# Longer read runs, a second queue at the start, and split first and last stores in a DMA-bound rotation kernel

## The chip, the core and the metric

The kernel runs on one core of a Trainium2 chip. The metric is device time in microseconds (us), the median of several runs. The profile comes from one further execution of each kernel; its span is about 1.8 us shorter than the time of that execution.

Engines in this text: DVE is the vector engine, which does the transposes. SP and ACT are the sync and scalar engines; here they only issue DMAs, each on a hardware queue of its own (q1 is SP's, q10 is ACT's in the profile). Sixteen DMA engines move the bytes of both queues.

## The reference

```python
def setup_inputs():
    batch, c, h, w = 32, 3, 256, 256
    return {"x": np.random.randn(batch, c, h, w).astype(np.float32)}

def reference(x):
    return np.rot90(x, k=1, axes=(-2, -1)).astype(np.float32)
```

96 images of 256 x 256 float32 are rotated: 25.17 MB are read and 25.17 MB are written. There is no arithmetic.

## The kernel before

Four images make a tile of 128 partitions x 2048 elements (8 KB of each partition, 1 MB in all). There are 24 tiles. Each is loaded with 8 KB runs, transposed on DVE with reversed access patterns, and stored with 8 KB runs.

```python
    in_pool = ctx.enter_context(tc.tile_pool(name="in_pool", bufs=12))
    out_pool = ctx.enter_context(tc.tile_pool(name="out_pool", bufs=12))

    for g in range(N // Q):                      # 24 tiles
        S = in_pool.tile([P, R * W], fp32, name="S")
        nc.sync.dma_start(out=S[:], in_=x_v[g])  # load, SP's queue
        U = out_pool.tile([P, R * W], fp32, name="U")
        # ... (the reversed views src of S and dst of U)
        nc.vector.transpose(dst, src)
        nc.scalar.dma_start(out=o_v[g], in_=U[:])  # store, ACT's queue
```

The scheduler gives the DMAs eight semaphores in turn, loads and stores together, in the order in which it schedules them. A DMA may be issued only when the DMA that held its semaphore before has landed. The compiled program shows it as waits. These are SP's loads in the kernel before (output of the build, semaphores numbered 0 to 7; the semaphores in the trace agree):

```
SP:  load 0 to load 4   no wait
     load 5             waits for semaphore 0   (load 0)
     load 6             waits for semaphore 2   (load 2)
     load 7             waits for semaphore 4   (load 3)
     load 8             waits for semaphore 6   (load 4)
     ...
```

In this program every load from load 5 on waits for an earlier load. The stores wait for earlier stores, except two (the fourth and the last but one), which take over the semaphore of a load that landed long before.

## Time and profile before

| | before |
|---|---|
| time, median of 3 runs | 124.34 us |
| profiled span | 122.7 us |
| DVE busy | 94.4 us (24 x 3.96 us) |
| bytes at the plateau of 427 GB/s | 117.9 us |

The page of the kernel before. In the slice rows each entry is one of 40 equal slices of the span; the first two rows are busy tenths.

```profile
span 122.7 us, 162 instructions
...
DVE  0199999999896696886976968879669688696600
...
DMA  3999999999999999999999999999999999999995
GB/s 88 419 427 411 312 430 433 422 433 427 427 427 427 427 427 427 427 427 427 427 427 427 427 427 427 427 427 430 427 427 427 427 427 427 427 427 427 427 427 211
...
DMA S<-in_x_dram 73%; DMA out_dram<-U 13%; DVE U L40 6%; SPq L35 1%; DVEq L40 0%
...
S<-in_x_dram SPq DMA_DIRECT2D x24, 1024.0 KB, 19.6
out_dram<-U ACTq DMA_DIRECT2D x24, 1024.0 KB, 16.5
```

The DMA engines are full from the second slice to the last but one: this kernel is bound by transfer. Only the first slice, the fifth (312 GB/s) and the last are low. The last two lines give the DMAs' median time from issue to landing.

### The profile page before, as it was taken

The page shows a single profiled execution, that of the slowest core. Times are in us where ns is not written, and L with a number is a line of the kernel's source. Part 1 is how long each engine was busy: PE and PEld are TensorE (multiplying, and loading weights), DVE is VectorE, ACT ScalarE, POOL GpSimd, SP SyncE. Part 2 cuts the span into 40 slices and gives each one's busy share as a digit, 9 for nine tenths or more (in the row PEclk, how much of TensorE's full clock was granted, in tenths as well). Part 3 has the DMA queues.
Part 4 walks back from the last instruction along what each step waited for, and adds up shares of the span by engine and source line. Part 5 has one row for each costly group of instructions (what it writes and reads, how often), then busy time and mean ns, then how long its engine had stood idle before and what let it go on. Part 6 is the DMA issues. An engine that isn't in the chain of part 4 may idle for free.

```text
span 122.7 us, 162 instructions
## 1 busy us (share of the span) xinstructions
DVE 94.4 (77%) x24; POOL 0.2 (0%) x4
## 2 busy tenths in 40 slices
DVE  0199999999896696886976968879669688696600
POOL 0000000000000000000000000000000000000000
DMA  3999999999999999999999999999999999999995
GB/s 88 419 427 411 312 430 433 422 433 427 427 427 427 427 427 427 427 427 427 427 427 427 427 427 427 427 427 430 427 427 427 427 427 427 427 427 427 427 427 211
DMA packets 6912, 50.33 MB, mean 410 GB/s; under 512 B 768, under 2 KB 768, under 8 KB 768
## 3 DMA queue, kind: packets, MB, share of 16 engines
q1 hardware_dynamic: 3456, 25.17, 49.6%
q10 hardware_dynamic: 3456, 25.17, 48.5%
HBM read 25.17 MB, written 25.17 MB: 410 GB/s over the span
## 4 chain that ended last, share of the span: by engine, by line
DMA 86%; DVE 6%; SPq 1%; issue 0%; DVEq 0%
DMA S<-in_x_dram 73%; DMA out_dram<-U 13%; DVE U L40 6%; SPq L35 1%; DVEq L40 0%
## 5 line engine op out<-in xcount | busy, mean ns | idle before, releaser
L40 DVE STREAM_TRANSPOSE U<-S 128x2048 f32<-128x2048 f32 x24 | 94.4, 3958 | 21.2 <-DMA S<-in_x_dram 20.2
L56 POOL MEMSET const-uint8-127<- 128x1 uint8 x1 | 0.1, 102 | 0.0
L56 POOL MEMSET const-bfloat16-1.0<- 128x1 bf16 x1 | 0.1, 101 | 0.0
L56 POOL MEMSET const-float32-0.0<- 128x1 f32 x1 | 0.1, 98 | 0.2 <-issue 0.2
L56 POOL MEMSET const-float32-1.0<- 128x1 f32 x1 | 0.1, 98 | 0.0
## 6 DMA issues: line engine op xcount, KB each, us to landing
S<-in_x_dram SPq DMA_DIRECT2D x24, 1024.0 KB, 19.6
out_dram<-U ACTq DMA_DIRECT2D x24, 1024.0 KB, 16.5
```

Of the source, the lines that this page charges most:

```text
L35: nc.sync.dma_start(out=S[:], in_=x_v[g])
L40: nc.vector.transpose(dst, src)
L56: nc = _bacc.Bacc("TRN2", target_bir_lowering=False, num_devices=1)
```

## The change

The intent: fewer, longer reads; a faster start through a second queue; finer first and last stores.

```diff
+    FOLD = 32
+    FIRST, LAST = 4, 2
+    xv = xf.rearrange("(n d f) -> n d f", n=G, d=FOLD)   # 32 runs of 32 KB
+    def load(dst, src):
+        nc.sync.add_instruction(mybir.InstDMACopy(
+            ins=[nc.sync.lower_ap(src, opt=False)],      # [32, 8192]
+            outs=[nc.sync.lower_ap(dst, opt=False)],     # [128, 2048]
+            queue="qSPDynamicHW", ... ))
...
-        nc.sync.dma_start(out=S[:], in_=x_v[g])
+        if n == 0:
+            nc.sync.dma_start(out=S, in_=xp[n])
+        elif n == 1:
+            nc.scalar.dma_start(out=S, in_=xp[n])
+        else:
+            load(S, xv[n])
...
-        nc.scalar.dma_start(out=o_v[g], in_=U[:])
+        pieces = FIRST if n == 0 else LAST if n == G - 1 else 1
+        f = F // pieces
+        for i in range(pieces):
+            nc.scalar.dma_start(
+                out=op[n, :, i * f : (i + 1) * f], in_=U[:, i * f : (i + 1) * f])
```

So tile 0 is stored by four DMAs of 256 KB in 2 KB runs, and tile 23 by two DMAs of 512 KB in 4 KB runs. The transpose walks the same elements in another order.

More of the change, by code (lines that the diff above doesn't have):

```diff
@@ L21 @@
     R = 8
-    K = H // R
-    Q = P // K
+    F = R * W
+    G = N // 4
+    FOLD = 32
+    FIRST, LAST = 4, 2
     fp32 = mybir.dt.float32
-    x_v = x.rearrange("b c (k r) w -> (b c k) (r w)", r=R).rearrange("(g p) f -> g p f", p=P)
-    o_v = out.rearrange("b c (k r) w -> (b c k) (r w)", r=R).rearrange("(g p) f -> g p f", p=P)
-    in_pool = ctx.enter_context(tc.tile_pool(name="in_pool", bufs=12))
-    out_pool = ctx.enter_context(tc.tile_pool(name="out_pool", bufs=12))
-    for g in range(N // Q):
-        S = in_pool.tile([P, R * W], fp32, name="S")
-        nc.sync.dma_start(out=S[:], in_=x_v[g])
-        U = out_pool.tile([P, R * W], fp32, name="U")
-        src = S.rearrange("p (r k q) -> p q r k", r=R, q=R)[:, ::-1, :, ::-1]
-        dst = U.rearrange("p (q k r) -> p q r k", q=R, r=R)
-        nc.vector.transpose(dst, src)
-        nc.scalar.dma_start(out=o_v[g], in_=U[:])
+    xf = x.rearrange("b c h w -> (b c h w)")
@@ new lines @@
+    of = out.rearrange("b c h w -> (b c h w)")
+    xp = xf.rearrange("(n p f) -> n p f", p=P, f=F)
+    op = of.rearrange("(n p f) -> n p f", p=P, f=F)
+    s_pool = ctx.enter_context(tc.tile_pool(name="S", bufs=12))
+    u_pool = ctx.enter_context(tc.tile_pool(name="U", bufs=12))
+    xv = xf.rearrange("(n d f) -> n d f", n=G, d=FOLD)
+    def load(dst, src):
+        nc.sync.add_instruction(
+            mybir.InstDMACopy(
+                name=nc.get_next_instruction_name(),
+                engine=mybir.EngineType.SP,
+                ins=[nc.sync.lower_ap(src, opt=False)],
+                outs=[nc.sync.lower_ap(dst, opt=False)],
+                queue="qSPDynamicHW",
+                mode="Copy",
+            )
+        )
@@ new lines @@
+    for n in range(G):
+        S = s_pool.tile([P, F], fp32, name="S")
+        U = u_pool.tile([P, F], fp32, name="U")
+        if n == 0:
[4 more added lines that the diff above has]
+            load(S, xv[n])
+        nc.vector.transpose(
+            U.rearrange("p (q k r) -> p r q k", q=R, r=R),
+            S.rearrange("p (r k q) -> p r q k", r=R, q=R)[:, :, ::-1, ::-1],
+        )
+        pieces = FIRST if n == 0 else LAST if n == G - 1 else 1
+        f = F // pieces
+        for i in range(pieces):
+            nc.scalar.dma_start(
+                out=op[n, :, i * f : (i + 1) * f], in_=U[:, i * f : (i + 1) * f]
+            )
```

## The prediction

> **What bounds it now.** The DMA engines. In the page's 40 slices the DMA row is 9 almost throughout, at 427 GB/s; 50.33 MB at 427 GB/s are 117.9 us of the 122.7 us span. DVE is busy 94.4 us (24 transposes of 3.96 us) and waits 20.2 us for loads: it follows. In the stretch table 14.5 to 110 us runs at 427 GB/s (loads and stores about 214 each, by the DMA records), and 110 to 121 us, stores alone, also at 427. So the tail is transfer too: the last store is issued at 115.6 us while earlier ones still run.
>
> The 4.8 us that are not full-rate transfer: (a) first issue at 0.73 us, first packet at 1.74, full rate from about 3.0; (b) 11.5 to 14.5 us runs at 314 instead of 427 GB/s, which loses 0.8 us. Load packets there take 400 to 700 ns instead of 309, and the first store, issued on ACT at 9.7 us, has its first packet at 13.9 us; no later store shows this. I take it for the cold start of the ACT queue. (c) 1.2 us after the last packet.
>
> **What the change does.**
> 1. Second load on ACT: ACT's queue starts cold at 0.7 us, beside SP's. If (b) is that cold start, it mostly overlaps (a). Worth at most 0.8 us; I take 0.6.
> 2. 22 loads read 32 KB runs: 2 read runs per engine for 8. An 8 KB packet starts every 306 ns; 256 beats of 32 B at 850 MHz are 301 ns. The Trainium skill, "DMA: Bandwidth & Descriptors", section "Why small descriptors are slow (HBM only)", gives about 3 cycles of overhead per packet, which agrees with the 5 ns here. Estimate: 22 x 6 x 5 ns = 0.65 us if packets count by reads; nothing if by the 8 KB writes. I take 0.4.
> 3. The same page ("Queues, rings and completion order") says that an engine switches queues at packet boundaries. With 32 KB load packets against 8 KB stores, loads may get far more than half: 214/214 would tilt towards 340/85, loads and DVE would end much earlier, and a long stretch of stores alone would follow. The bytes are the same and some queue always has work, so this moves time and saves none. Semaphores keep at most 4 loads and 4 stores in flight.
> 4. First store in four pieces of 2 KB runs, last in two of 4 KB: 24 + 8 more packets per engine, 5 ns each: costs 0.15 us; the extra issues on ACT (0.34 us each) are hidden.
> 5. The transpose's access order changes, same 2048 elements; DVE has slack, so even 10% would be hidden.
>
> Sum: -0.6 - 0.4 + 0.15, and some -0.3 for a faster start with two queues issuing: about -1.2 us, nearly all on the critical resource, since every byte waits for it.
>
> **Prediction.** 123.1 us, 80% range 122.0 to 124.3. Faster by over 2% (below 121.85): 0.10. Within 2%: 0.87. Slower by over 2%: 0.03.
>
> **What would show it.** Step 1: no slice of about 312 GB/s near 12 us. Step 2: fewer, 32 KB load packets, and a plateau of 430 to 433. Step 3: uneven shares, loads landed well before 110 us, DVE done earlier. Step 4: still about 1.2 us after the last packet. Step 5: transposes near 3.96 us.
>
> **What would make it wrong.** If 32 KB reads into 4 partitions lose the spread over the engines or stall writes, the plateau falls and it is slower. If the reads' overhead were larger than 5 ns, the plateau could reach 435 and the time fall to 121. If the dip belongs to the first writes to DRAM rather than to the queue, step 1 gains nothing.

The 5 ns per packet in this text are an assumption of the prediction. The traces give about 3.7 ns (see step 2 at the end).

## More of the kernel before

What SP's queue waits for, in the kernel before (total us, times, longest us):

```profile
SPq L35 <- DMA S<-in_x_dram: 81.8, 19, 4.6
SPq L67 <- DMA out_dram<-U: 29.5, 4, 22.3
```

The first line is the semaphore waits of the loads: each waits for a load, and loads land regularly. The second is the wait at the end of the program (line 67 is the launch, not a load).

## The result, and the profile after

| | before | after |
|---|---|---|
| time, median of 6 runs each | 124.35 us | 125.34 us (125.02 to 125.83) |
| ratio | | 1.0085, 95% interval 1.0062 to 1.0109 |
| profiled span | 122.7 us | 123.9 us |

A ratio is the mean time of one kernel's fast runs over that of the other's fast runs of the same rounds, so it is not quite the ratio of the medians. The change makes the kernel 0.85% slower: clear of the noise, but within 2%. The prediction was 123.1 us, with a range that ended at 124.3.

The same lines of the page, after:

```profile
span 123.9 us, 168 instructions
...
DVE  0039999999999999999999999918999993000000
...
DMA  3999979999999999999999999999999999999992
GB/s 87 423 505 413 434 244 412 378 436 442 436 439 436 428 410 399 450 407 442 439 423 452 439 423 439 386 391 428 428 428 426 434 423 426 426 428 431 423 414 118
...
DMA out_dram<-U 56%; DVE U L62 17%; DMA S<-in_x_dram 6%; DVEq L97 3%; DVEq L62 0%; ACTq L69 0%
...
S<-in_x_dram SPq DMA_DIRECT2D x23, 1024.0 KB, 13.1
out_dram<-U ACTq DMA_DIRECT2D x22, 1024.0 KB, 10.8
```

The low fifth slice is gone. In its place are low slices at the sixth (244) and the eighth (378). A packet counts where it starts, so slices with 32 KB packets scatter (505 is such an artefact). DVE ends much earlier, and the chain now runs through stores: the loads are done at 83 us, not 111.

To avoid that artefact I spread each DMA record evenly over its duration, and added up the time lost against 428 GB/s. Loss = length of the stretch x (1 - rate / 428). The last column is a run explained below.

| stretch, us | before | after | first store whole |
|---|---|---|---|
| 0 to 3.5 | 2.68 | 2.64 | 2.52 |
| 3.5 to 15 | 0.89 | 0.04 | 0.07 |
| 15 to 24 | 0.02 | **1.40** | 0.35 |
| 24 to 118 | 0.12 | 0.03 | 0.02 |
| 118 to the end | 1.41 | **2.21** | 1.44 |
| sum | 5.12 | 6.32 | 4.40 |

The start gains nothing. The dip before the first store moved from 11.5 to 15 us with the first store itself. Between 18 and 24 us there is a new loss, and the end is longer: the sixteen engines' last completion records lie 0.55 us apart before (121.01 to 121.56) and 1.28 us apart after (121.32 to 122.60). If each engine has a fixed share of the bytes, the one that lost most ends last. The kept records carry no engine number, so this was not checked.

What happens at 18 to 24 us is told by the waits of SP's queue and by its issues. First its waits, after:

```profile
SPq L97 <- DMA out_dram<-U: 51.8, 1, 51.8
SPq L40 <- DMA S<-in_x_dram: 47.4, 15, 7.6
SPq L40 <- DMA out_dram<-U: 10.8, 3, 8.5
```

The third line is new: loads (line 40) wait three times, up to 8.5 us, for a **store**. Then SP's issues between 5 and 19 us and between 19 and 21 us, after (start, length, what, count):

```profile
10.59 0.47 SPq L40 DMA_DIRECT2D S<-in_x_dram  x1
...
19.62 1.77 SPq L40 DMA_DIRECT2D S<-in_x_dram  x2
```

From 11.1 to 19.6 us SP issues nothing. The load at 10.59 is load 5; the one at 19.62 is load 6. The compiled program says why:

```
SP after:  load 0, 2, 3, 4   no wait          (load 1 is on ACT)
           load 5            semaphore 2  (load 2)
           load 6            semaphore 4  (piece 0 of the first store)
           load 7            semaphore 6  (piece 2 of the first store)
           load 8            semaphore 0  (piece 3 of the first store)
```

Piece 0 was issued at 12.14 us, and the last of its 16 completions came at 19.61 us. Load 6 followed at 19.62, and its first packet came at 23.0 us. But the load queue had emptied at 18.5 us: no load packet runs from 18.5 to 23.0 us. In the last part of this gap the store packets that ran alone became slow. The records of one DMA engine, joined by their times (start ns, length ns; the 2 KB packets of the pieces are left out):

```
13796  1251  load, 32 KB
15047  1236  load, 32 KB
16273  1696  load, 32 KB      slow: the first pieces begin
20475   309  store, 8 KB
20781   309  store, 8 KB
21087   309  store, 8 KB
21393   309  store, 8 KB
21699   309  store, 8 KB
22004   384  store, 8 KB      slow, although no other queue runs
22384   434  store, 8 KB
22815   381  store, 8 KB
23199  1572  load, 32 KB      load 6 begins
```

### The profile page after: what moved, and what is told of

The parts are those of the page before. It is cut to its first block, busy times and chain, and to the rows that moved or that the text cites. A ratio compares the mean times of both kernels' runs of the same rounds, so it can differ in the third digit from the quotient of the medians.

```text
span 123.9 us, 168 instructions
## 1 busy us (share of the span) xinstructions
DVE 92.3 (74%) x24; POOL 0.2 (0%) x4
## 4 chain that ended last, share of the span: by engine, by line
DMA 62%; DVE 17%; DVEq 3%; issue 0%; ACTq 0%
DMA out_dram<-U 56%; DVE U L62 17%; DMA S<-in_x_dram 6%; DVEq L97 3%; DVEq L62 0%; ACTq L69 0%
## 5 line engine op out<-in xcount | busy, mean ns | idle before, releaser
L62 DVE STREAM_TRANSPOSE U<-S 128x2048 f32<-128x2048 f32 x24 | 92.3, 3945 | 11.1 <-DMA S<-in_x_dram 8.1
## 6 DMA issues: line engine op xcount, KB each, us to landing
out_dram<-U ACTq DMA_DIRECT2D x22, 1024.0 KB, 10.8
```

Source lines behind the costliest of these rows:

```text
L62: nc.vector.transpose(U.rearrange("p (q k r) -> p r q k", q=R, r=R), S.rearrange("p (r k q) -> p r q k", r=R, q=R)[:, :, ::-1, ::-1],)
```

## The experiments

Sixteen kernels ran, all correct. "Gap" is the longest stretch of at least 1 us without a load packet before the last load ends, from the DMA records. Times are medians.

| run | time, us | ratio to before | gap in the loads, us |
|---|---|---|---|
| before | 124.35 | | none |
| after | 125.34 | 1.0085 | 18.5 to 23.0 |
| e1 first store whole | 123.78 | 0.9948 | none |
| e2 no 32 KB runs | 125.71 | 1.0101 | 18.7 to 22.7 |
| e3 load 1 on SP | 125.30 | 1.0069 | 16.4 to 21.1 |
| e4 last store whole | 125.34 | 1.0077 | 18.2 to 22.8 |
| e5 first store one DMA, 2 KB runs | 123.90 | 0.9955 | none |
| e6 first store four DMAs, 8 KB runs | 123.99 | 0.9968 | none |
| b2 before + four pieces | 125.70 | 1.0103 | 16.4 to 20.5 |
| b3 before + 32 KB loads | 123.96 | 0.9964 | none |
| e7 pieces, six loads ahead | 124.67 | 1.0021 | 23.5 to 28.2 |
| e9 pieces, eight loads ahead | 124.59 | 1.0018 | 31.2 to 36.8 |
| e8 no pieces, loads 5 and 6 late | 124.23 | 0.9987 | none |
| e11 no pieces, load 5 very late | 125.09 | 1.0053 | 15.4 to 17.8 |
| e10 whole, eight ahead | 123.81 | 0.9960 | none |
| b7 before, eight ahead | 124.36 | 1.0002 | none |
| b5 before, three input buffers | 126.38 | 1.0169 | none |
| b6 before, one queue | 125.14 | 1.0063 | none |

### First: which part of the change costs

Theory A: the four pieces of the first store. Theory B: the 32 KB packets. Each run undoes one part.

**e1**, first store whole.

```diff
-    FIRST, LAST = 4, 2
+    FIRST, LAST = 1, 2
```

> The changed kernel with its first store in one piece. Theory A (the four pieces of 2 KB runs crowd out the sixth load and bring on the second slow stretch at 21 to 24 us, which also leaves the 16 engines' ends 1.3 us apart): about 124.0 us, no second slow stretch, engines end within 0.7 us of each other. Theory B (the 32 KB load packets themselves slow the stretch and scatter the engines): unchanged, 125.3 us, engines still over 1.2 us apart.

Measured: 123.78 us (123.73 to 123.82), 0.5% faster than before. The engines end 0.52 us apart. Theory A holds: the pieces cost 1.6 us, and without them the change is a gain. Waits of SP's queue in this run:

```profile
SPq L97 <- DMA out_dram<-U: 55.7, 4, 48.4
SPq L40 <- DMA S<-in_x_dram: 52.5, 18, 5.6
SPq L40 <- DVE U L62: 0.9, 2, 0.4
```

No load waits for a store any more.

The table of stretches shows 14 to 24 us too (the stretch, its length, DVE busy, POOL busy, clock, DMA share, GB/s). The kernel before:

```profile
14.00:24.00 10.00, 10.00 (x3) 0.00 (x0) 1.00 1.01 423
```

The changed kernel:

```profile
14.00:24.00 10.00, 10.00 (x4) 0.00 (x0) 1.00 0.99 352
```

And e1:

```profile
14.00:24.00 10.00, 10.00 (x4) 0.00 (x0) 1.00 0.99 406
```

The DMA share hides the difference (0.99 in both of the last two), because a slow packet counts as busy. The rate shows it.

**e2**, all loads in 8 KB runs.

```diff
-            load(S, xv[n])
+            nc.sync.dma_start(out=S, in_=xp[n])
```

> The changed kernel with all loads in 8 KB runs. Theory A: still slow, 125.2 to 125.6 us (the 0.3 us of the longer packets is lost, the crowding stays). Theory B: 124.3 us or less, engines end within 0.6 us, no stretch under 400 GB/s after 19 us.

Measured: 125.71 us, and the gap is there. Theory B falls. The 32 KB runs are worth about 0.4 us (125.71 - 125.34) in this setting.

**e3**, the second load back on SP.

```diff
-            nc.scalar.dma_start(out=S, in_=xp[n])
+            nc.sync.dma_start(out=S, in_=xp[n])
```

> The changed kernel with the second load back on the sync queue. The prediction's step 1 (cold ACT queue) would have the dip before the first store larger by 0.6 us and the time at 125.9; if the dip belongs to the first store whatever the queue did before, the dip stays 0.7 to 0.8 us and the time within 0.2 us of 125.3.

Measured: 125.30 us. The loss from 11 to 15 us is 0.72 us there, against 0.71 us from 15 to 18.5 us in the changed kernel. So an ACT queue that has already carried a load does not spare the dip: it comes with the first store, and the second load's queue is worth nothing. That refutes step 1 of the prediction. It agrees with the Trainium skill, "DMA: Bandwidth & Descriptors", section "Issuing engines are not separate DMA queues", which says that DMAs of all issuing engines run on the same 16 DMA engines and that a second one saves only the time to issue. In the changed kernel the first landing is even later, because two loads share the engines: DVE begins at 8.12 us, against 5.57 in e3 and 5.72 before. The comparison of e3 with the changed kernel has the gap on both sides. Without a gap, e1 and b3 below differ by 0.18 us (123.78 against 123.96) in the second load's queue, the split last store and the order of the transpose together, so the second queue may be worth up to about that there.

**e4**, last store whole.

```diff
-    FIRST, LAST = 4, 2
+    FIRST, LAST = 4, 1
```

> The changed kernel with its last store in one piece of 8 KB runs. 8 more packets of 5 ns per engine are 0.04 us and one DMA fewer completes: 125.3 us, within 0.1. If the two last DMAs add to the tail, 124.9 or less.

Measured: 125.34 us (124.91 to 125.91). The two last pieces are worth nothing either way.

### Second: what in the four pieces costs

**e5**, one DMA that moves the same 2 KB runs.

```diff
+        if n == 0:     # one DMA on ACT
+            ins=[nc.scalar.lower_ap(U.rearrange("p (i f) -> p i f", f=f), opt=False)]
+            outs=[nc.scalar.lower_ap(op[n].rearrange("p (i f) -> p i f", f=f), opt=False)]
```

> The changed kernel with its first store as ONE DMA that still moves 2 KB runs (512 of them). It separates what the four pieces cost: if the 2 KB packets (their number) crowd the sixth load out, 125.0 to 125.4 us, as with four pieces, and the sixth load starts near 23 us; if the number of DMAs handed to the scalar queue does, about 123.9 us (0.12 us for the small packets above the whole store), and the sixth load starts directly after the fifth, near 18 us.

Measured: 123.90 us. Small packets alone do not cost it.

**e6**, four DMAs in 8 KB runs.

```diff
+        if n == 0:
+            for i in range(4):
+                nc.scalar.dma_start(out=op[n, i::4, :], in_=U[i::4, :])
```

> The changed kernel with its first store as FOUR DMAs of 256 KB in 8 KB runs (every fourth partition). The mirror of the run before: if the number of DMAs crowds the load out, about 125.2 us and the sixth load starts after 22 us; if the 2 KB packets do, 123.8 to 124.0 us and it starts near 18 us.

Measured: 123.99 us. Four DMAs alone do not cost it either. Both of my either-or readings had failed. In e1, e5 and e6 the loads up to load 5 are issued by 3 us and load 6 near 9.3 us. In the changed kernel load 5 goes at 10.6 and load 6 at 19.6. The scheduler had handed out the semaphores in another order. In e6 six loads took theirs in the first eight, in the changed kernel only five, and the next load inherited that of a piece.

**b2**, the kernel before with the four pieces only.

```diff
-        nc.scalar.dma_start(out=o_v[g], in_=U[:])
+        pieces = 4 if g == 0 else 1
+        f = R * W // pieces
+        for i in range(pieces):
+            nc.scalar.dma_start(out=o_v[g][:, i * f : (i + 1) * f], in_=U[:, i * f : (i + 1) * f])
```

> The kernel before with nothing but the four pieces of the first store. If the pieces alone make the loss, whatever the load's runs: 124.4 + 1.4 = about 125.7 us. If they hurt only together with the 32 KB loads or the second load on the scalar queue: 124.4 to 124.6 us.

Measured: 125.70 us, as theory A said: the pieces hurt by themselves, with 8 KB loads too. Again loads wait for the store (11.4 us in 3 waits), and the gap is there. But most of the 1.3 us is lost elsewhere. This is the row of rates of b2's page, to be compared with that of the kernel before:

```profile
GB/s 85 426 423 431 306 408 404 431 426 428 431 423 431 423 423 433 428 426 431 428 426 428 426 423 431 428 428 431 428 423 431 426 423 431 428 428 428 428 291 211
```

The last slice but one has 291 GB/s instead of 427. By the spread records, the stretch from 3.5 to 24 us loses 0.35 us more than before, and that from 118 to 121 us 0.98 us more. The late loads shift the rest of the program: the last load lands at 115.1 us instead of 111.5, the last store is issued at 119.2 instead of 115.6, and by then the stores before it are nearly done, so the engines run short of work. In the changed kernel the loads are done at 83 us and this does not happen; its loss at the end goes mostly with the uneven ends. So b2 confirms the delay of the loads, not the same sum of losses.

**b3**, the kernel before with the 32 KB loads only.

```diff
+        if g >= 2:     # the raw copy of the change, SP's queue
+            ins=[nc.sync.lower_ap(xv[g], opt=False)], outs=[nc.sync.lower_ap(S, opt=False)]
```

> The kernel before with nothing but the 32 KB loads (from the third on). From the packets' measured spacing (1217 ns for 32 KB, 1224 ns for four of 8 KB, 44 per engine) 0.3 us: 124.05 us; with the leave-one-out difference of the two runs above (125.34 - 125.71) 0.4 us. The prediction had 0.4. If longer packets unbalance the engines, 124.4 or more.

Measured: 123.96 us, ratio 0.9964 (0.9951 to 0.9977): about 0.45 us of gain, close to the predicted 0.4.

### Third: is it the load queue running dry

Theory C: the pieces harm only through their semaphores, which make a load late, so that the load queue runs dry. Theory D: four DMAs of 2 KB packets harm as such.

**e7**, all pieces kept, but six loads scheduled before them. The edit hoists the loads and adds an ordering for the scheduler, which is no wait in the program.

```diff
+    for n in range(AHEAD):          # AHEAD = 7
+        fetch(n)
...
+            tc.keep_in_program_order(s)
+            if n == 0:
+                tc.add_manual_dep(s.ins, loads[5].ins.name, <order only>, reason="order")
```

> The changed kernel with its four 2 KB pieces kept, but scheduled after load 5 (an order for the scheduler, no wait), so that six loads, not five, take their semaphores before the pieces do; load 5 is then issued near 3 us instead of 10.6, load 6 near 10.6 instead of 19.6. Theory C (the pieces harm only by taking the eight DMA semaphores, so that loads 5 to 8 are issued late and the sync queue runs dry from 18 to 23 us): 123.9 to 124.1 us, no stretch without load packets before 60 us. Theory D (four DMAs of 2 KB packets together harm by themselves): 125.2 us or more.

Measured: 124.67 us, between the two. The gap was not removed, it moved to 23.5 to 28.2 us: load 8 now held the semaphore of piece 0, which landed at 24.15 us; so load 8 was issued at 24.16 us, and its first packet came at 28.2 us. Waits of SP's queue in e7:

```profile
SPq L40 <- DMA S<-in_x_dram: 46.1, 14, 6.9
SPq L40 <- DMA out_dram<-U: 9.1, 2, 8.2
```

Piece 0 took 12.1 us to land here. Its 2 KB packets get one or two turns after each 32 KB load packet: 84 ns against 1,240 in the records (medians). The better the loads run, the later a small store piece lands, and the load behind it pays.

**e8**, no pieces, but loads 5 and 6 made late through their buffers.

```diff
-        S = s_pool.tile([P, F], fp32, name="S")
+        S = (t_pool if n in (0, 1, 5, 6) else s_pool).tile([P, F], fp32, name="S")
```

> The kernel with the first store whole (123.78 us), but loads 5 and 6 put into the buffers of tiles 0 and 1, so that they are issued late, near 11.7 and 15.5 us, as the pieces made them. Theory C: the sync queue runs dry near 18 us and the time rises by 0.5 us or more, to 124.3 to 125.3. Theory D: no piece is there, 123.8 us.

Measured: 124.23 us (124.05 to 124.31). That is 0.45 us slower than e1 without any piece, just short of the 0.5 that I had expected at least, and no full gap opened. It counts for theory C, weakly.

After these runs the theory was likely but not shown: every run with a gap had pieces.

**e9**, pieces kept, eight loads ahead of them.

```diff
-    AHEAD = 7
+    AHEAD = 8
-                    loads[5].ins.name,
+                    loads[7].ins.name,
```

> The changed kernel, all four 2 KB pieces and the two last ones kept, but scheduled so that eight loads take their semaphores before the first piece does. Theory C: no gap in the load packets before 60 us, 123.9 to 124.1 us. Theory D: 125 us or more though the loads never run dry. If a gap only moves once more, 124.6.

Measured: 124.59 us, the third of the three outcomes. The gap moved once more, to 31.2 to 36.8 us: load 11 was issued at 32.78 us, when the third piece had landed at 32.77 us.

Waits of SP's queue in e9:

```profile
SPq L40 <- DMA S<-in_x_dram: 42.5, 11, 10.9
SPq L40 <- DMA out_dram<-U: 10.7, 2, 8.3
```

So I found no schedule of the four pieces without a gap, and theory C was not confirmed from this side. What e9 adds is that the loss travels with the gap: from 3.5 to 30 us it loses 0.15 us in all, although the pieces are issued from 12.3 us on and the last lands at 33.7 us; from 30 to 40 us it loses 0.68 us. How long the gap is does not set the loss: 4.6 us of gap stand beside 1.6 us lost in the changed kernel, 5.6 us beside 0.8 in e9 (both against e1).

**e11**, no pieces, and load 5 alone forced to be very late.

```diff
-        S = s_pool.tile([P, F], fp32, name="S")
+        S = (t_pool if n in (1, 5) else s_pool).tile([P, F], fp32, name="S")   # t_pool: 1 buffer
```

> The kernel with the first store whole (123.78 us), no pieces, but load 5 put into the buffer of tile 1, so that it is issued near 15.5 us, when the fifth load is nearly done. Theory C: the load packets have a gap of 3 to 5 us near 18 us, and the time is 124.5 to 125.3. Theory D: 123.8 us.

Measured: 125.09 us (124.15 to 125.73), 1.3 us above e1. The one thing that differs is a load that waits for DVE (and the loads that queue behind it on SP), as the waits of SP's queue in e11 show:

```profile
SPq L41 <- DMA S<-in_x_dram: 49.1, 16, 6.4
SPq L41 <- DVE U L63: 7.0, 3, 6.3
```

The profiled execution is the fastest of the six (124.15 us); its gap, 15.4 to 17.8 us, is shorter than I had expected. The scatter is wide. In this execution the stretch of the gap shows no extra loss (0.31 us from 15 to 24 us, against 0.35 in e1); it is 0.37 us slower than e1 in all. No slow execution was profiled. So it is shown that a late load costs time without any piece, in all six runs; that the dry queue makes the whole 1.3 us of the median is argued, not seen. Theory D had 123.8 us here and falls as the whole explanation; e9's loss before 30 us leaves little for the pieces by themselves.

### Fourth: the dip before the first store, and a better version

**b5**, the kernel before with three input buffers.

```diff
-    in_pool = ctx.enter_context(tc.tile_pool(name="in_pool", bufs=12))
+    in_pool = ctx.enter_context(tc.tile_pool(name="in_pool", bufs=3))
```

> The kernel before with 3 input buffers instead of 12: when the first store is issued near 9.7 us only the end of one load is still queued. If the 4.1 us from the issue of the first store to its first packet are the backlog of loads queued ahead of it, they shrink to under 2 us; if a first store always takes 4 us, they stay, and the engines run dry meanwhile. The time is not predicted better than 124 to 127 us.

Measured: 126.38 us over 4 runs. With little queued ahead the first store's first packet came 2.3 us after its issue (9.59 to 11.87 us), against 4.1 us before (9.73 to 13.88). The backlog is thus part of the delay, not all of it: inconclusive between my two readings.

**b6**, the kernel before with everything on SP's queue.

```diff
-        nc.scalar.dma_start(out=o_v[g], in_=U[:])
+        nc.sync.dma_start(out=o_v[g], in_=U[:])
+        if g + AHEAD < G:               # AHEAD = 5; loads 0 to 4 before the loop
+            load(g + AHEAD)
```

> The kernel before with loads and stores all issued on the sync queue (five loads ahead). If the slow stretch of 11.5 to 14.5 us is the start of a second queue beside a busy one, it is gone: 0.7 us less, 123.7 us, if nothing else is lost. If it belongs to the first writes to DRAM, it stays near the first store: 124.4 us.

Measured: 125.14 us, slower than either branch had it. The slow packets before the first store are there (loss from 11 to 15 us 0.75 us, then 0.36 to 18.5 us). So the dip is not the start of a second queue. It goes with the first store. Why is open: in e5, e7 and e9, whose first store has 2 KB runs and more loads queued behind, the loss from 11 to 18.5 us is only 0.08 us.

**e10**, a candidate for the best: 32 KB loads, eight ahead, first and last store whole.

```diff
-    FIRST, LAST = 4, 2
+    FIRST, LAST = 1, 1        # on top of e9
```

> Candidate for the best: eight loads ahead, 32 KB loads, first and last store whole. If a deep backlog of loads also shields from the slow packets before the first store (as in the two runs that had none there), 123.3 to 123.5 us; if not, as with six ahead, 123.8.

Measured: 123.81 us. Depth adds nothing to e1's 123.78; of the two expectations, the second.

**b7**, the same with 8 KB loads and load 1 on SP.

```diff
-            nc.scalar.dma_start(out=S, in_=xp[n])
+            nc.sync.dma_start(out=S, in_=xp[n])
-            loads[n] = load(S, xv[n])
+            loads[n] = nc.sync.dma_start(out=S, in_=xp[n])
```

> The same as the candidate, but with 8 KB loads throughout and the second load on the sync queue: the kernel before with eight loads ahead. It gives the worth of the 32 KB loads and of the depth apart: 124.3 us if depth is worth nothing by itself, 123.8 if it removes the slow stretch (0.7 us) there.

Measured: 124.36 us, the same as before. More depth by itself is worth nothing, and the 32 KB runs are worth 0.5 us beside it (with the smaller edits of e10).

The best version is e1: the change with its first store whole, 123.78 us, ratio 0.9948 (0.9936 to 0.9960).

## Why the prediction was wrong, point by point

- **Bound by DMA: right.** The bytes at 428 GB/s are 117.6 us of either span; what differs is the time lost beside them, 5.12 us before and 6.32 after.
- **Step 1, "If (b) is that cold start, it mostly overlaps (a) ... I take 0.6": wrong.** Worth 0 in the changed kernel (e3: 125.30 against 125.34). The dip came with the first store although ACT's queue had carried a load before. The prediction named this way to fail ("If the dip belongs to the first writes to DRAM"); b6 agrees with it, but the cause inside the hardware is not shown. The faster start (0.3 us) was wrong too: 2.68 us lost up to 3.5 us before, 2.64 after.
- **Step 2, longer reads, 0.4 us: right.** 0.37 us by e2 against the changed kernel, 0.45 us by b3. The trace has 704 load packets of 32 KB. The Trainium skill, "DMA: Bandwidth & Descriptors", section "Why small descriptors are slow (HBM only)", gives some 3 cycles of overhead per packet; 32 KB packets run at 1,213 ns alone, against 4 x 306 = 1,224 ns for four of 8 KB, so 11 ns are saved for three packets fewer, some 3.7 ns each. A fixed cost per packet agrees with that; no run here shows the length of a cycle. Beside stores it was less (about 1,220 ns). The size was partly luck: 0.4 was a choice between the 0.65 worked out and nothing. I had the plateau at 430 to 433; it is 431 to 432 only where loads run alone, and 428 to 430 with stores.
- **Step 3, arbitration: right in direction.** The page's section "Queues, rings and completion order" says that an engine switches between queues at packets. A packet there holds several descriptors, about 9 to 17 as a rule; the prediction took it for one record of the profile. In the records a 32 KB load packet goes with one or two 8 KB store packets (299 to 395 from 30 to 60 us): in that stretch loads run at about 320 and stores at 110 GB/s, and the last load ends at 83.0 us instead of 110.8. That tilt alone costs nothing: b3 and e1 have it and are faster than before.
- **Step 4, "costs 0.15 us": this is the step that failed.** It cost 1.6 us (125.34 against 123.78). I counted packets, and left out what I had written one step earlier about semaphores. The four pieces take four of the eight; one load fewer than in e1 is ahead when they start, and loads 6, 7 and 8 may go only when a piece has landed. Measured chain: piece 0 lands at 19.61 us, load 6 is issued at 19.62, its first packet is at 23.0, while the load queue is empty from 18.5. Seven runs with such a gap (e11 without any piece among them) and the changed kernel itself took 124.59 to 125.71 us; the runs with 32 KB loads and no gap took 123.78 to 124.23. The loss has two parts: 1.05 us more from 15 to 24 us than in e1 (1.40 - 0.35), of which 0.31 fall before the load queue is empty and about 0.75 after, and 0.77 us at the end (2.21 - 1.44), where the engines' ends are 1.28 us apart instead of 0.52. Taken together they are 1.82 us of these two profiled runs. That the pieces cost 1.6 us and delay the loads is shown; that the delay alone makes the whole sum is not.
- **The split last store: right.** No effect beyond the scatter (e4).
- **Step 5, transposes: right.** 3,945 ns against 3,958. DVE stands in the chain of the page with 17%, but its last transpose ended at 103 us, and stores alone kept the DMA engines full from there to 120 us.
- **The sum.** With step 1 and the faster start at 0, step 2 at -0.4 and the pieces at +1.6, one gets 124.35 + 1.2 = 125.55 us; 125.34 was measured.

What stays open: why an empty queue takes some 4 us to its first packet, why packets of the other queue slow down meanwhile, why the first store brings a dip in some runs and hardly in others, and why gaps of 4.6 to 5.6 us cost anything from 0.8 to 1.6 us with 32 KB loads.

## What to carry to other kernels

Before a DMA is split into pieces, count the completion semaphores: with a fixed ring of them, as here, each piece is also a place that a later load must wait for, and a small piece in competition with large packets lands late. In the profile look for a load that waits for a store in the waits of the issuing queue; in this case 10.8 us of it stood beside 1.6 us lost, on a kernel whose DMA engines looked busy throughout. Price each part of a change also by whom it can delay, and measure the parts one by one: here one part hid the gain of another.

## What the Trainium skill lacked or had wrong

- "DMA: Bandwidth & Descriptors", section "Latency and other measured facts", gives about 600 ns to the first byte for a DMA issued from the sync or scalar engine. At the idle start it was 1.0 us here from the start of the issue (0.73 to 1.74), and 0.64 us from its end (1.10), which is close to the page. What it lacks is the case beside a busy queue: 4.1 us from the start of the issue for the first store before, and 3.4 us for load 6 after.
- The same page does not say that the packets of a busy queue slow down while another DMA is starting: from 11.5 to 13.9 us half of the 8 KB load packets in the kernel before took over 410 ns (up to 733) instead of 309, and from 22 to 23.1 us most store packets in the changed one took 360 to 450 ns.
- The same page says that queues take turns by packets, but not that the length of the runs then sets the shares: 214 and 214 GB/s with 8 KB on both sides, about 320 and 110 with 32 KB loads against 8 KB stores.
- The same page does not say what a read run longer than the write run is worth. A load that reads 32 KB and writes it to four partitions shows as one packet of 32 KB, and saved about 0.4 us here in 22 loads.
- No page has the cost of a queue that runs dry while the other has work: 0.68 us in e9 between 30 and 40 us, where its gap lies. In e11 the medians differ from e1 by 1.3 us, but the one profiled execution by only 0.37.
